# One row of inverse lengths by way of DRAM, and four places for residual tiles, in a two-layer trunk kernel

## The chip, the cores and the metric

The kernel runs on one core of a Trainium2 chip. Its time is the device time of one execution in microseconds. The core has five engines with instruction queues of their own: TensorE (PE; its weight loads are listed apart as PEld), VectorE (DVE), ScalarE (ACT), GpSimd (POOL) and SyncE (SP), which here issues nearly all DMA transfers. Each queue is worked off in order.

## The reference, cut to what matters

The trunk has two layers over 1024 positions of width 1024. The first layer's mixer joins a gated MLP over chunks with a gated delta rule; the second layer's mixer is a differential attention with 8 heads. After its mixer each layer has an MLP and a gated side input. All is in float32.

```python
def rms_norm(x, gain):
    xf = x.astype(jnp.float32)
    y = xf * lax.rsqrt(jnp.mean(xf * xf, axis=-1, keepdims=True) + NORM_EPS)
    return (y * gain.astype(jnp.float32)).astype(x.dtype)

...
        if layer % 2 == 0:
...
            h = h + jnp.concatenate([a_out, b_out], axis=-1) @ w_out_e[i]
        else:
...
            h = h + o @ w_out_o[i]
        hn = rms_norm(h, ln_mlp[layer])
        h = h + jnp.square(jax.nn.relu(hn @ w_mlp1[layer])) @ w_mlp2[layer]
        gate = jax.nn.sigmoid(rms_norm(h, ln_ple[layer]) @ w_ple_gate[layer])
        h = h + (p[layer] @ w_ple_proj[layer]) * gate
```

The change touches two things in this: the factor `rsqrt(mean(...))` of the normalization ahead of the first MLP, for the first half of the positions, and the addition `h + o @ w_out_o` of the second mixer, for the second half of the positions.

## The kernel before

**Layout.** Features lie on the 128 partitions and positions along the free dimension, in two halves of 512 positions (`HT`). The residual stream `h` lies in DRAM (`h_dram`) as eight tiles of 128 features by 1024 positions. Weights are loaded in pieces (`raw`, 8 places), and each piece is split into a high and a low part (`w`, 12 places): ScalarE makes the high part (L230) and VectorE the low part (L234). Each product is three matmuls, high by high, low by high and high by low (`mm3`). A matmul of 128 by 512 adds into one PSUM bank, and a bank is free again when VectorE has added it to its tile.

**Order.** A scheduler orders the instructions of each engine when the program is built, by its own estimate of times. That estimate includes the DMAs, so a step that is made another way can move its neighbours too. Each DMA on SP waits in the queue for what it needs, and all behind it wait too.

**First mixer's end.** `mix_out` multiplies the mixed heads by the output weights, one half of the positions after the other, eight output tiles `m` of 24 matmuls each. For each `m` it adds the bank to the residual tile (`acc`, L1343), adds its square to the running sums (`sqs`, L253 to L257) and stores the tile. After the first half it calls `rms`: four matmuls with a column of ones sum `sqs` over the partitions (tile `aux`), VectorE makes the mean (`ms`, L273) and GpSimd the inverse length `r` (L275), 512 numbers, 4 on each partition. What follows needs them as a row of 512 on every partition (`rb`). `rms` has two ways for that. The near way multiplies `r`, broadcast, by the identity matrix (four matmuls into `aux`, with `r` and `ident` as operands) and copies the bank on ScalarE (L287). The far way stores `r` to DRAM in the order of positions (`rd`, L279) and loads it back to all partitions (L281); three other calls use it. Then VectorE scales each of the eight tiles of the first half with gain and `rb` (L1354), ScalarE casts the high part (`hi`, L1358) and VectorE takes the low part (`lo`, L1359). The MLP's first products read these.

While the first half ends, the second half's last heads are still coming in: four transposes (`pab`, L83) each, then a cast on ScalarE (`ahi`, L1665) and the low part on VectorE (`alo`, L1666). The second half's out-projection reads them.

**Attention's end.** The second mixer's out-projection is made in parts: heads 0 to 5 of the first half of the positions and heads 0 to 4 of the second half are multiplied while the last attention blocks still run (`mix_part`, called for `h` 0 and then 1), and the other heads after the attention (`mix_out` with `k0` 6 and 5). `mix_part` loads a residual tile (`res`, L1298) one output tile ahead, adds the bank (L1310) and stores it back to DRAM (L1311). The tiles `res` take turns in the places `c0` and `c1`. The places `c0` to `c3` hold q tiles of the attention: `c0` and `c1` for even heads, `c2` and `c3` for odd heads, so the last head (7) has `c2` and `c3`. After the last value product of head 7 its two halves are transposed and split (`ohi` L1194, `olo` L1195).

Of the kernel before, what the change touches and what calls it, by code (L numbers as in the profile page):

```python
# [11 lines left out]
F32 = mybir.dt.float32  # L12
# [6 lines left out]
P = 128  # L19
# [4 lines left out]
HT = 512  # L24
# [19 lines left out]
def f32(ap):  # L44
    return ap.bitcast(F32)
# [73 lines left out]
class Trunk:  # L119
# [1170 lines left out]
    def mix_part(self, h, n, w_out, h_dram):  # L1290
        nc = self.nc
        cols = slice(h * HT, (h + 1) * HT)
        res = []

        def load():
            if len(res) < KT:
                res.append(self.slot(f"c{len(res) % 2}", [P, HT], F32, "res"))
                nc.sync.dma_start(res[-1], h_dram[len(res) - 1, :, cols])  # L1298

        load()  # L1300
        for m in range(KT):
            if m % 2 == 0:
                w = self.weight(w_out[0 : n * P, m * P : (m + 2) * P], n, 256)
            load()
            ps = self.mm_ps()
            for k in range(n):
                self.mm3(ps, w.at(k, slice((m % 2) * P, (m % 2 + 1) * P)), self.mixed[h][k], k == 0, k == n - 1)
                if k % 2:
                    yield
            nc.vector.tensor_tensor(res[m], res[m], ps, ALU.add)  # L1310
            nc.sync.dma_start(h_dram[m, :, cols], res[m])  # L1311


    def mix_out(self, h, acc, w_out, h_dram, gain_next, k0=0, late=0):

        nc = self.nc
        cols = slice(h * HT, (h + 1) * HT)
        n = KT - k0
        wide = 256 if n == KT else 512
        pss, place = {}, {}  # L1320

        order = [(m, i) for m in range(KT) for i in range(n)]
        if late:
            order[: 2 * n] = sorted(order[: 2 * n], key=lambda o: (o[1] >= n - late, o))
        for m, i in order:
            ml = m % (wide // P)
            if i == 0:
                if ml == 0:
                    w = self.weight(w_out[k0 * P :, m * P : m * P + wide], n, wide, per=512 // wide)
                a = place[m] = acc(m)  # L1330
                nc.sync.dma_start(a, h_dram[m, :, cols])
                pss[m] = self.mm_ps()
            a, ps = place[m], pss[m]
            k = (i + late) % n
            if h == 1 and k0 and (m, i) == (5, 0):

                self.pe.floor = self.rb_mark
            self.mm3(ps, w.at(k, slice(ml * P, (ml + 1) * P)), self.mixed[h][k0 + k], i == 0, i == n - 1)
            self.pe.floor = None
            if i < n - 1:  # L1340
                yield
                continue
            nc.vector.tensor_tensor(a, a, ps, ALU.add)  # L1343
            self.add_square(h, a)
            nc.sync.dma_start(h_dram[m, :, cols], a)
            yield
        self.sqs_last = self.sqs[h]
        if h == 0:
            self.rb[0] = self.rms(0, self.sqs[0])[1]
            self.rb_mark = self.pe.mark  # L1350
            lows = []
            for m in range(KT):
                a = acc(m)
                inst = nc.vector.scalar_tensor_tensor(a, a, gain_next[:, m : m + 1], self.rb[0], ALU.mult, ALU.mult)  # L1354
                if m > 1:
                    self.pe.behind(inst, lows[m - 2])
                hi, lo = self.hs_new[0][m] = self.hs_parts(0, m)
                nc.scalar.copy(hi, a)  # L1358
                lows.append(nc.vector.tensor_tensor(lo, a, f32(hi), ALU.subtract).ins.name)  # L1359
        yield  # L1360
# [858 lines left out]
```

## Time and profile before

| | us |
|---|---|
| median of 3 executions | 2503.18 (2501.72 to 2505.22) |
| the profiled execution | 2504.11 |
| its span, first to last instruction | 2502.4 |
| TensorE busy in the span | 2491.0 |
| VectorE busy | 1811.0 |
| ScalarE busy | 1312.9 |

The 1.7 us between the profiled execution's time and its span lie around the span. Times in the quoted rows are microseconds from the span's start, with the start first and the length second. In rows of waits, "A <- B" says that A waited for B, with the total, the number of times and the longest. In rows of stretches, each engine's busy time stands with its number of instructions, then the clock granted to TensorE (1.00 is full), the DMA engines' busy share and GB/s.

### The profile page before, as it was taken

The numbers are of one execution on the slowest core, as the hardware profiler recorded it, in microseconds if no ns is written. First come the engines' busy times: TensorE is split into PE (matmuls) and PEld (weight loads), VectorE is DVE, ScalarE is ACT, GpSimd is POOL, SyncE is SP. The second block draws the span as 40 slices with busy tenths as digits, with TensorE's granted clock in tenths as the row PEclk, the third lists the DMA queues.
The fourth block names the chain that finished last, engine by engine and source line by source line (L and its number), as shares of the span: only waits on it lengthen the run. The fifth ranks groups of instructions, "written<-read, shape, count | busy, mean of one in ns | idle before, by whom it ended". The sixth has DMA issues, their size and how long they took to land.

```text
span 2502.4 us, 39882 instructions
## 1 busy us (share of the span) xinstructions
PE 2491.0 (100%) x13905; PEld 2139.8 (86%) x13905; DVE 1811.0 (72%) x3542; ACT 1312.9 (52%) x2669; POOL 284.9 (11%) x267
## 2 busy tenths in 40 slices
PE   9999999999999999999999999999999999999999
PEld 7898998888888888888999999988888888888887
DVE  7868665787666877656577877776887656787576
ACT  6635473555555444534466666654654555445452
POOL 0211220000000000000444444410000000000000
PEclk9999999999999999999999999999999999999999
DMA  8464435467547756543211111367466548656651
GB/s 241 125 185 106 148 125 184 137 208 242 190 160 272 243 165 211 187 134 130 77 56 55 52 52 60 110 209 235 141 219 229 188 166 294 202 189 203 198 177 64
DMA packets 318835, 410.81 MB, mean 164 GB/s; under 512 B 45765, under 2 KB 181929, under 8 KB 318633
## 3 DMA queue, kind: packets, MB, share of 16 engines
q1 hardware_dynamic: 318072, 407.73, 50.8%
q8 instruction: 109, 1.79, 0.3%
q14 instruction: 94, 0.76, 0.1%
q10 hardware_dynamic: 560, 0.53, 0.1%
HBM read 295.95 MB, written 112.20 MB: 163 GB/s over the span
## 4 chain that ended last, share of the span: by engine, by line
PE 96%; DVE 2%; DMA 1%; issue 0%; ACT 0%; POOL 0%; SPq 0%; DVEq 0%; ACTq 0%
PE mm L80 83%; PE po L80 3%; PE qk L80 2%; PE aux L80 2%; PE tr L83 2%; DVE lg L1128 1%; DVE lg L1139 0%; PE pks L80 0%; PE pkq L80 0%; PE pvn L80 0%; PE pkk L80 0%; PE pgm L80 0%; DMA h_dram<-res 0%; PE pab L83 0%; DMA x<-in_x_dram 0%
## 5 line engine op out<-in xcount | busy, mean ns | idle before, releaser
L230 ACT CAST w<-raw 128x512 fp32r<-128x512 f32 x598 | 366.8, 617 | 466.9 <-PE mm L80 411.6
L80 PE MATMUL mm<-g,w 128*128 128x512 f32 x2592 | 601.0, 394 | 0.0
L80 PEld LDWEIGHTS mm<-g,w 128*128 128x128 f32 x2592 | 486.8, 188 | 113.0
L80 PE MATMUL mm<-hi,w 128*128 128x512 f32 x1728 | 554.2, 395 | 0.0
L80 PE MATMUL mm<-w,hi 128*128 128x256 f32 (+2 forms) x2528 | 507.4, 295 | 0.9 <-DVE k L1030 0.9
L234 DVE TENSOR_TENSOR w<-raw,w 128x512 fp32r<-128x512 f32 x534 | 367.3, 694 | 194.6 <-ACT w L230 183.0
L80 PEld LDWEIGHTS mm<-w,hi 128*128 128x128 f32 x2528 | 401.2, 188 | 13.9 <-issue 1.2
L80 PEld LDWEIGHTS mm<-hi,w 128*128 128x128 f32 x1728 | 324.5, 188 | 73.7 <-ACT u L386 0.4
L80 PE MATMUL mm<-w,lo 128*128 128x256 f32 (+2 forms) x1264 | 370.2, 294 | 0.0
L80 PE MATMUL mm<-lo,w 128*128 128x512 f32 x864 | 340.3, 394 | 0.0
L80 PE MATMUL mm<-t,w 128*128 128x512 f32 x1152 | 271.2, 394 | 0.0
L80 PEld LDWEIGHTS mm<-t,w 128*128 128x128 f32 x1152 | 216.5, 188 | 50.5
L80 PEld LDWEIGHTS mm<-w,lo 128*128 128x128 f32 x1264 | 238.2, 189 | 5.5
L80 PEld LDWEIGHTS mm<-lo,w 128*128 128x128 f32 x864 | 162.5, 188 | 36.0
L275 POOL TENSOR_TENSOR r<-ms,mhalf 128x4 f32<-128x4 f32 x12 | 14.1, 1173 | 1507.7 <-DVE ms L273 1478.6
L234 DVE TENSOR_TENSOR g<-graw,g 128x512 fp32r<-128x512 f32 x216 | 147.7, 685 | 6.5 <-DMA gd<-g 5.0
L230 ACT CAST g<-graw 128x512 fp32r<-128x512 f32 x216 | 132.7, 617 | 22.9 <-DMA gd<-g 11.8
L1131 ACT ACTIVATE lg<-lg,nm 128x256 f32<-128x256 f32 (+7 forms) x128 | 99.1, 775 | 69.7 <-DVE nm L1128 67.9
L370 ACT ACTIVATE g<-g 128x512 f32<-128x512 f32 x100 | 63.0, 631 | 82.1 <-DVE g L304 81.8
L1128 DVE CUSTOM_DVE_ANT_0 lg<-qk,al 128x512 f32<-128x512 f32 (+3 forms) x128 | 74.6, 589 | 36.8 <-PE qk L80 32.8
L234 POOL TENSOR_TENSOR w<-raw,w 128x512 fp32r<-128x512 f32 x64 | 84.1, 1332 | 76.3 <-ACT w L230 51.5
L80 PE MATMUL mm<-ohi,w 128*128 128x512 f32 x256 | 85.5, 405 | 2.4 <-DVE res L1310 2.3
(360 smaller groups left out, 3577.5 us busy)
## 6 DMA issues: line engine op xcount, KB each, us to landing
raw<-in_w_mlp_dram SPq DMA_DIRECT2D x352, 256.0 KB, 3.3
graw<-gd SPq DMA_DIRECT2D x224, 256.0 KB, 2.7
gd<-g SPq DMA_DIRECT2D x192, 256.0 KB, 3.3
raw<-in_w_ple_gate_dram SPq DMA_DIRECT2D x76, 256.0 KB, 3.6
acc<-h_dram SPq DMA_DIRECT2D x64, 256.0 KB, 4.8
keep<-in_w_mlp_dram SPq DMA_DIRECT2D x64, 256.0 KB, 4.9
raw<-in_w_in_e_dram SPq DMA_DIRECT2D x60, 256.0 KB, 3.7
h_dram<-acc SPq DMA_DIRECT2D x48, 256.0 KB, 2.7
```

The lines of the kernel that those rows point to most:

```text
L80: self._next(self.engine.matmul(*a, **k))
L83: self._next(self.engine.transpose(*a, **k))
L230: inst = self.nc.scalar.copy(hi, src)
L234: inst = (lo_engine or self.nc.vector).tensor_tensor(lo, src, f32(hi), ALU.subtract)
L275: nc.gpsimd.tensor_tensor(r, ms, self.mhalf[:, 0:4], ALU.pow)
L370: nc.scalar.activation(g, src, AF.Relu)
L1128: nc.vector.tensor_tensor_reduce(out=lg[:, k0:k1], in0=ps[:, : k1 - k0], in1=al[:, u0 + k0 : u0 + k1], scale=-1.0, scalar=3.0e38 if c == 0 ...
L1131: nc.scalar.activation(lg[:, :n], lg[:, :n], AF.Exp, bias=nm[:, r, nch - 1 : nch], scale=-1.0, accum_out=me.sums[:, b, r : r + 1])
```

## The change

`mix_out` asks for the far way where `k0` is 0, that is in the first mixer; the second mixer's call keeps the near way. In `mix_part` the residual tiles of the second half of the positions (`h` 1) take turns in four places, `c0` to `c3`; the first half keeps two.

```diff
@@ mix_part
         def load():
             if len(res) < KT:
-                res.append(self.slot(f"c{len(res) % 2}", [P, HT], F32, "res"))
+                res.append(self.slot(f"c{len(res) % (4 if h else 2)}", [P, HT], F32, "res"))
                 nc.sync.dma_start(res[-1], h_dram[len(res) - 1, :, cols])
@@ mix_out
         if h == 0:
-            self.rb[0] = self.rms(0, self.sqs[0])[1]
+            self.rb[0] = self.rms(0, self.sqs[0], far=not k0)[1]
             self.rb_mark = self.pe.mark
             lows = []
```

What the far way is in `rms`:

```python
        if rows and far:
            d = self.dp.tile([4, P], F32, name=self.nm("rd"))
            nc.sync.dma_start(d.rearrange("t p -> p t"), r)
            rb = self.sp.tile([P, HT], F32, tag=f"rb{half}", name=self.nm("rb"), bufs=1)
            nc.sync.dma_start(rb, d.rearrange("t p -> (t p)").partition_broadcast(P))
```

The scheduler's order moves with it at the first place. Names end in running numbers, which are lower by 3 in the changed kernel from here on, since it has four matmuls and a copy less and two DMAs more. VectorE at the end of the first half, before:

```order
L273 TENSOR_SCALAR ms_4933<-aux_4928 128x4
L234 TENSOR_TENSOR w_5231<-raw_5228,w_5230 128x512
L1354 SCALAR_TENSOR_TENSOR acc_4384<-acc_4384,cols,rb_4942 128x512 x2
L1666 TENSOR_TENSOR alo_5014<-pab_5008,ahi_5013 128x512
L234 TENSOR_TENSOR w_5237<-raw_5234,w_5236 128x512
L1359 TENSOR_TENSOR lo_4946<-acc_4384,hi_4945 128x512
```

And VectorE at the same place now, up to the addition that empties the first bank of the second half:

```order
L273 TENSOR_SCALAR ms_4933<-aux_4928 128x4
L1666 TENSOR_TENSOR alo_5011<-pab_5005,ahi_5010 128x512
L1354 SCALAR_TENSOR_TENSOR acc_4384<-acc_4384,cols,rb_4939 128x512 x2
L1666 TENSOR_TENSOR alo_5029<-pab_5023,ahi_5028 128x512
L1359 TENSOR_TENSOR lo_4943<-acc_4384,hi_4942 128x512
...
L234 TENSOR_TENSOR w_5234<-raw_5231,w_5233 128x512
L1343 TENSOR_TENSOR acc_5077<-acc_5077,mm_5079 128x512
```

The first `alo` moved ahead of the two L1354, which read the row `rb`; the second `alo` now follows right behind them (it came after two more of them and two splits before), and the weights' split `w_5228` moved behind them. Between the second `alo` and the L1343 stand ten instructions: four L1359, four L1354 and two L234.

TensorE at the same place, before:

```order
L80 MATMUL aux_4928<-ones,sqs_4484 128x1 x4
...
L80 MATMUL aux_4937<-ident,r_4935 128x128 x4
L83 MATMUL pab_5008<-ident,qkv_2756 128x128 x4
...
L83 MATMUL pab_5026<-ident,qkv_2756 128x128 x4
```

And now, where 18 matmuls stand between the two sets of transposes, 27 between the second set and the first reader of `alo_5029`, and 22 from that reader to the first matmul into `mm_5251`, whose bank is the one that `mm_5079` had:

```order
L80 MATMUL aux_4928<-ones,sqs_4484 128x1 x4
L83 MATMUL pab_5005<-ident,qkv_2756 128x128 x4
...
L83 MATMUL pab_5023<-ident,qkv_2756 128x128 x4
...
L80 MATMUL mm_5079<-alo_5029,w_5073 128x512
...
L80 MATMUL mm_5251<-ahi_4724,w_5227 128x512
```

The four matmuls with `r` are gone, the first transposes moved up to the sums, and a part of the fourth output tile's matmuls moved behind the first reader of `alo_5029`.

SP at the same place now:

```order
L105 DMA raw_5330<-in_w_out_e_dram 128x2x256
L279 DMA rd_4937<-r_4935 128x4x1
L281 DMA rb_4939<-rd_4937 128x512
L1331 DMA acc_5249<-h_dram 128x512 x4
L352 DMA raw_5461<-in_w_mlp_dram 128x2x256
```

The two DMAs stand behind the last weight tile of the out-projection; the MLP's first weight tile (`in_w_mlp`) came ahead of the four residual loads before.

SP at the attention's end, before; the last residual tile is `res_19093`:

```order
L1298 DMA res_19035<-h_dram 128x512
L1331 DMA acc_19364<-h_dram 128x512
L1311 DMA h_dram<-res_18997 128x512
L105 DMA raw_19434<-in_w_out_o_dram 128x512
L1298 DMA res_19055<-h_dram 128x512
L1331 DMA acc_19237<-h_dram 128x512 x4
L1331 DMA acc_19446<-h_dram 128x512
L105 DMA raw_19440<-in_w_out_o_dram 128x512
L1311 DMA h_dram<-res_19035 128x512
L352 DMA raw_19574<-in_w_mlp_dram 128x2x256
L1311 DMA h_dram<-res_19055 128x512
L1298 DMA res_19093<-h_dram 128x512
```

And now, where the last residual tile is `res_19090` and the store four tiles before it is that of `res_18953`:

```order
L1298 DMA res_19052<-h_dram 128x512
L105 DMA raw_19355<-in_w_out_o_dram 128x512
L1311 DMA h_dram<-res_18953 128x512
L1331 DMA acc_19361<-h_dram 128x512
L105 DMA raw_19425<-in_w_out_o_dram 128x512
L1298 DMA res_19090<-h_dram 128x512
L1331 DMA acc_19361<-h_dram 128x512
L1311 DMA h_dram<-res_18994 128x512
```

The load of the last residual tile moved ahead of the stores of the three tiles before it. The orders of TensorE and VectorE are the same there before and now.

## The prediction

> **What bounds the kernel now.** I read the page, then what TensorE waits for, then the chain of work that ended last at the two places of the change, then each engine's instructions there in order of time.
>
> ```profile
> PE 2491.0 (100%) x13905; PEld 2139.8 (86%) x13905; DVE 1811.0 (72%) x3542; ACT 1312.9 (52%) x2669; POOL 284.9 (11%) x267
> ...
> PE 96%; DVE 2%; DMA 1%; issue 0%; ACT 0%; POOL 0%; SPq 0%; DVEq 0%; ACTq 0%
> ```
>
> TensorE is busy for 2491.0 of 2502.4 us. A microsecond by which TensorE is put off is a microsecond of the kernel; what another engine gains is worth nothing unless TensorE waits for it. Its waits:
>
> ```profile
> PE mm L80 <- DVE res L1310: 2.3, 1, 2.3
> ...
> PE mm L80 <- DVE acc L1343: 0.2, 1, 0.2
> ```
>
> The first, its longest in the program, lies at the second place (residual tiles); the second is the only one at the first place (inverse lengths). So the second edit has something to win; the first has almost nothing to win and must not open a wait.
>
> **First edit: the row by way of DRAM.** The chain at the place, from the sums of squares (`aux`, 423.55) on:
>
> ```profile
> 423.55 0.79 PE aux L80 x8
> 424.34 5.89 PE mm L80 x25
> 430.23 0.89 PE aux L80 x8
> 431.12 0.44 PE pab L83 x4
> ...
> 433.39 4.90 PE mm L80 x21
> ...
> 441.91 29.25 PE mm L80 x125
> ```
>
> TensorE never stands still: a matmul starts every 0.2345 us (5.89 for 25, 4.90 for 21). Removed: the four broadcasting matmuls, 0.89 us of TensorE (the row at 430.23), and the copy that followed on ScalarE, which lies beside TensorE and saves nothing. The other engines:
>
> ```profile
> 425.16 1.01 POOL L275 TENSOR_TENSOR r<-ms,mhalf 128x4 f32<-128x4 f32 x1 [58.94 <-DVE ms L273]
> ```
> ```profile
> 431.78 1.42 DVE L1354 SCALAR_TENSOR_TENSOR acc<-acc,cols,rb 128x512 f32<-128x512 f32 x2 [1.04 <-ACT rb L287]
> ...
> 436.18 0.75 DVE L1354 SCALAR_TENSOR_TENSOR acc<-acc,cols,rb 128x512 f32<-128x512 f32 x1
> 436.84 0.69 DVE L1666 TENSOR_TENSOR alo<-pab,ahi 128x512 fp32r<-128x512 f32 x1
> 437.44 0.68 DVE L234 TENSOR_TENSOR w<-raw,w 128x512 fp32r<-128x512 f32 x1
> ```
>
> GpSimd has r at 426.17 and VectorE uses the row at 431.78, 5.6 us later. (Between starts on VectorE: 0.66 us after an L1354, 0.60 after the others.) Added: two DMAs on SP, r to DRAM and back to all partitions. Three other places of this kernel do the same, and one shows it undisturbed:
>
> ```profile
> 1109.43 1.01 POOL L275 TENSOR_TENSOR r<-ms,mhalf 128x4 f32<-128x4 f32 x1 [41.71 <-DVE ms L273]
> ```
> ```profile
> 1110.46 0.37 SPq L279 DMA_DIRECT2D rd<-r  x1
> 1118.92 0.34 SPq L281 DMA_DIRECT2D rb<-rd  x1
> ```
> ```profile
> L279 SPq DMA_DIRECT2D rd<-r x3: 366/370/387, 39.8 to 1110.5; - x3
> ...
> DMA to landing us min/median/max: 8.4/8.4/8.4
> ```
> ```profile
> L281 SPq DMA_DIRECT2D rb<-rd x3: 320/338/339, 50.4 to 1118.9; - x3
> ...
> DMA to landing us min/median/max: 5.5/5.5/5.5
> ```
>
> The first DMA lands 8.4 us after its issue and the second 5.5, at all three places alike; here the second leaves 8.46 after the first. So r at 426.2 gives the second DMA at 434.65, the row at 440.15, and the first L1354 at 440.2: 14.0 us after r, and 8.4 later than before.
>
> What queues behind that wait: on VectorE, in order, the two L1354 and then the lower part of the last transposed head (`alo`, L1666), which the out-projection reads. It starts at 440.2 + 2 x 0.66 = 441.5 and ends 0.69 later, at 442.2. TensorE has, between the sums (end 424.34) and its first use of that tile, two sets of four transposes (0.44 each) and by the new order 18 and 27 matmuls: 424.34 + 0.88 + 45 x 0.2345 = 435.8. There it stops for 6.4 us.
>
> Then come 22 matmuls (5.2 us: 447.4) up to the first into a new PSUM bank, which VectorE has to empty first (L1343). In the new order `alo`, four L1359 and two L234 (0.60 each) and four L1354 (0.66 each) start ahead of that L1343: 441.5 + 6.84 = 448.4, its end 449.05. So that matmul starts at 449.1 instead of 441.91: **+7.2 us**, the 0.89 counted in. A slower clock after the gap (below) takes some 1.5 us from those 22 matmuls, which then end at 448.9, still under the same wait.
>
> Two queues more. SP stands from 426.2 to 434.65: the four residual loads behind it leave at 435 (before: 433.5) and are first used after 24 more matmuls, past 454; the MLP's first weight tile waits for its place until VectorE's split at 445 (before: issued at 430.8) and is used after the 96 matmuls left of this projection, at 449.1 + 22.5 = 471.6. Both have 10 us and more to spare. On ScalarE the next weight cast moves behind two `hi` casts, to 442.3; that is inside the VectorE chain above. Nothing later gives the 7.2 us back, because from 441.91 on the chain before is TensorE alone.
>
> **Second edit: four residual tiles.**
>
> ```profile
> 1725.13 6.67 DMA h_dram<-res
> 1731.81 0.02 issue
> 1731.82 2.92 DMA res<-h_dram
> ```
> ```profile
> 1712.68 0.38 SPq L1311 DMA_DIRECT2D h_dram<-res  x1
> ...
> 1717.44 0.32 SPq L1298 DMA_DIRECT2D res<-h_dram  x1
> ```
> ```profile
> 1729.82 0.69 DVE L234 TENSOR_TENSOR w<-raw,w 128x512 fp32r<-128x512 f32 x1 [0.70 <-PE mm L80]
> 1734.87 0.69 DVE L1310 TENSOR_TENSOR res<-res,mm 128x512 f32<-128x512 f32 x1 [4.35 <-DMA res<-h_dram]
> ```
> ```profile
> 1732.86 0.40 PE L80 MATMUL mm<-ohi,w 128*128 128x512 f32 x1
> 1735.61 0.79 PE L80 MATMUL mm<-ohi,w 128*128 128x512 f32 x1 [2.35 <-DVE res L1310]
> ...
> 1738.97 0.63 PE L80 MATMUL mm<-ohi,w 128*128 128x512 f32 x2
> ```
> ```profile
> 1735.00:1736.00 1.00, 0.39 (x1) 0.39 (x2) 1.00 (x2) 0.00 (x0) 0.00 (x0) 0.64 0.80 252
> 1736.00:1737.00 1.00, 1.00 (x3) 0.77 (x3) 1.00 (x3) 0.00 (x0) 0.00 (x0) 0.50 0.87 270
> 1737.00:1738.00 1.00, 1.00 (x4) 0.75 (x3) 1.00 (x2) 0.55 (x1) 0.00 (x0) 0.50 1.04 379
> 1738.00:1739.00 1.00, 1.00 (x5) 0.79 (x4) 0.44 (x2) 0.67 (x2) 0.00 (x0) 0.65 1.01 365
> 1739.00:1740.00 1.00, 1.00 (x6) 0.83 (x5) 1.00 (x3) 0.72 (x2) 0.00 (x0) 1.00 0.98 372
> ```
>
> The last residual tile takes the place of the one two before it, so its load waits for a store that lands 6.67 us after its issue. VectorE's addition waits for the load (4.35 us), and TensorE for the bank that this addition empties. With four places the load waits only for the store four tiles back (issued 1712.68), and in the new order it stands ahead of the next store, at about the place of the 1717.44 load: landed long before VectorE is free at 1730.4. The bank is then empty at 1731.1 and TensorE goes on at 1733.1.
>
> The gain is more than the 2.35 us of waiting, since the granted clock (the third figure from the right, in slices of 1 us) is at 0.50 for 0.72 + 2 + 0.70 = 3.4 us after the gap and 1.00 again at 1739. By counting: between 1732.86 and 1738.97 nine matmuls start, in 6.11 us instead of 9 x 0.2345 = 2.11: **-4.0 us**. The Trainium skill, "TensorE: Matmul & The Clock Gate", section "Why this matters for your kernels", asks for no TensorE gaps above about 3 us; by it this 2.35 us gap would leave the clock alone, and the sum below would be +4.8. The row at 0.50 decides against that.
>
> The extra places held the last head's q tiles; their last transposes are done before either load is due, and no DMA wait on SP grows. VectorE's and TensorE's orders are unchanged here. Late next would be the bank behind it, freed by the `olo` two instructions later on VectorE, at 1732.4, before its matmul at 1734.5. The other loads of this part leave earlier, which nothing uses.
>
> **Sum.** +7.2 - 4.0 = +3.2 us on the profiled execution's 2504.11, 0.9 above the median of 2503.18; against the median 2506.4, which I round to **2506.5**. 0.2%, or 5.0 us, is about what a measurement of this kernel can tell from no change.
>
> **Rivals.**
>
> *Faster.* One mechanism: a short round trip. The shortest frequent DMA here:
>
> ```profile
> graw<-gd SPq DMA_DIRECT2D x224, 256.0 KB, 2.7
> ```
>
> Two at 2.7 us give the row at 431.6, as early as now. TensorE then meets no wait, 0.89 + 0.16 are saved at the first place and 4.0 at the second: 2498.1. It decides from a row at 433.7 on (no gap); the two edits cancel with a row at 437.0. Against it stand the three equal landings at 8.46 and 5.5: 512 single words written apart, unlike a 256 KB tile. Chance 0.06. The Trainium skill, "DMA: Bandwidth & Descriptors", section "Anatomy of one DMA — SWDGE (gpsimd) path", gives about 2.0 us fixed per DMA (for the GpSimd path, where this queue is SP's); an estimate from it, 4 us for both, would put the row at 430.2, the same case. The trace's 14.0 us speaks against it.
>
> *Slower by more than 5 us.* The clock after the 6.4 us gap stays at half for two stretches of 3.4 us (the length seen at the second place). Then the 22 matmuls lose 3.4 us, not 1.5, and end at 450.8: +8.9 - 4.0 = +4.9; half a microsecond more in the DMAs makes it 2508.9. Or SP's order at the second place brings another late load and only the 2.35 us, or nothing, comes back: +4.8 to +7.2, up to 2510.4. For it: the gap is nearly three times the one seen; against it: one stretch was enough there. Chance 0.36.
>
> *The edits do nothing.* The new order has the two DMAs and the early loads; no chance of its own.
>
> **How the numbers follow.** My forecast, within 0.2%, has 0.58: +2 to +5, from 7.2 to 8.2 at the first place and 3.5 to 5.2 at the second (the 2.35 us of waiting, and a clock at half for 2 to 5.4 us, an estimate: 0.6 to 1.6 stretches of 3.4, since the gap may end anywhere in one). The range adds the scatter of the executions before (2501.7 to 2505.2) below and the slower case above: 2502.5 to 2510.5.
>
> **What would show it.** Right: rb leaves SP 8.5 us after rd near 434.7; TensorE stands about 6.4 us near 436, released by `alo` L1666, with a granted clock of 0.5 behind it; the wait for `res` L1310 near 1735 is gone and the clock stays 1.00 there. Wrong: no gap near 436 (a short round trip), a gap well over 7 us, or TensorE waiting near 1735 again.

## The result, and the profile after

| | before | now |
|---|---|---|
| median | 2503.32 (16 executions, 2501.72 to 2506.73) | 2509.00 (16 executions, 2507.55 to 2510.44) |
| the profiled execution | 2504.11 | 2507.87 |
| its span | 2502.4 | 2506.2 |

All in us. The ratio is 1.0021, with a 95% interval of 1.0015 to 1.0027. That is slower, by about as much as a measurement of this kernel can tell. It lies 2.5 us above the forecast of 2506.5.

TensorE's waits in the changed kernel (in total, times, longest):

```profile
PE mm L80 <- DVE alo L1666: 5.4, 1, 5.4
...
PE aux L80 <- DVE ms L273: 0.3, 1, 0.3
PE mm L80 <- DVE w L234: 0.3, 1, 0.3
```

The wait for `res` (L1310) is gone. A wait for `alo`, more than twice as long, has come. The chain of work at the first place:

```profile
424.82 1.02 POOL r L275
425.84 0.02 issue
425.86 7.54 DMA rd<-r
...
433.46 5.53 DMA rb<-rd
438.99 0.02 issue
439.02 1.41 DVE acc L1354 x2
440.43 0.61 DVE alo L1666
441.05 0.04 issue
441.09 36.41 PE mm L80 x147
477.50 0.56 PE aux L80 x6
```

GpSimd's r is there at 425.84, the row on all partitions at 438.99: 13.2 us for the trip. Then come two scalings and the low part that was queued behind them, and only then TensorE. The clock granted to TensorE there (third figure from the right, stretches of 2 us):

```profile
438.00:440.00 2.00, 0.00 (x0) 0.00 (x0) 0.98 (x2) 0.20 (x1) 0.00 (x0) 0.68 1.01 365
440.00:442.00 2.00, 0.91 (x2) 0.82 (x3) 2.00 (x4) 1.56 (x3) 0.00 (x0) 0.50 0.36 139
442.00:444.00 2.00, 2.00 (x6) 1.52 (x6) 2.00 (x4) 1.02 (x2) 0.00 (x0) 0.50 0.00 0
444.00:446.00 2.00, 2.00 (x7) 1.54 (x6) 2.00 (x5) 1.28 (x4) 0.00 (x0) 0.61 0.28 79
446.00:448.00 2.00, 2.00 (x10) 1.63 (x9) 2.00 (x5) 1.82 (x5) 0.00 (x0) 1.00 0.15 52
```

At half clock for 1.28 + 2 + 2 + 1.56 = 6.8 us, of which TensorE works only from 441.09 on. The second place, on VectorE and in the same view:

```profile
1736.71 0.68 DVE L1310 TENSOR_TENSOR res<-res,mm 128x512 f32<-128x512 f32 x1
```
```profile
1736.00:1738.00 2.00, 2.00 (x13) 1.64 (x12) 1.90 (x4) 1.38 (x3) 0.00 (x0) 1.00 0.85 313
```

The last L1310 follows the split ahead of it without idle time, and the clock stays at 1.00.

To see where the time went, I cut each profiled execution at three moments that every kernel has: TensorE's first matmul of the sums at the end of the first mixer's first half (A), the same at the end of its second half (B), and the first such matmul at the end of the second mixer's first half (C). In us, worked out from the starts of those matmuls:

| kernel | A to B | B to C | C to the end |
|---|---|---|---|
| before | 47.61 | 1284.57 | 746.84 |
| now | 53.91 | 1280.56 | 748.27 |
| difference | +6.30 | -4.01 | +1.43 |

A to B holds the first place, B to C the second. The third column was in no term of the forecast.

### The profile page after: what moved, and what is told of

Read it like the earlier page. It is cut to its first block, busy times and chain, and to the rows that moved or that the text cites. A ratio compares the mean times of both kernels' runs of the same rounds, so it can differ in the third digit from the quotient of the medians.

```text
span 2506.2 us, 39867 instructions
## 1 busy us (share of the span) xinstructions
PE 2492.6 (99%) x13897; PEld 2139.0 (85%) x13897; DVE 1808.8 (72%) x3542; ACT 1313.6 (52%) x2668; POOL 285.3 (11%) x267
## 4 chain that ended last, share of the span: by engine, by line
PE 94%; DVE 3%; DMA 2%; issue 1%; ACT 0%; POOL 0%; SPq 0%; DVEq 0%; ACTq 0%
PE mm L80 81%; PE po L80 3%; PE qk L80 2%; PE aux L80 2%; PE tr L83 2%; DMA raw<-in_w_ple_gate_dram 1%; DVE lg L1128 1%; DVE lg L1139 0%; DMA h_dram<-xt 0%; DMA rd<-r 0%; DVE w L234 0%; PE pks L80 0%; PE pkq L80 0%; PE pkk L80 0%; PE pvn L80 0%
## 5 line engine op out<-in xcount | busy, mean ns | idle before, releaser
L234 DVE TENSOR_TENSOR w<-raw,w 128x512 fp32r<-128x512 f32 x534 | 365.6, 691 | 194.3 <-ACT w L230 184.0
L234 DVE TENSOR_TENSOR g<-graw,g 128x512 fp32r<-128x512 f32 x216 | 147.2, 683 | 5.3 <-DMA gd<-g 5.2
L234 POOL TENSOR_TENSOR w<-raw,w 128x512 fp32r<-128x512 f32 x64 | 84.1, 1333 | 76.5 <-ACT w L230 51.6
L80 PE MATMUL mm<-ahi,w 128*128 128x512 f32 x256 | 84.0, 405 | 0.2 <-ACT ahi L1665 0.2
```

Of the source, the lines that this page charges most:

```text
L80: self._next(self.engine.matmul(*a, **k))
L234: inst = (lo_engine or self.nc.vector).tensor_tensor(lo, src, f32(hi), ALU.subtract)
```

## The experiments

The medians stand against those of the kernel before on the same chip: 2502.74 for the first four, 2503.04 for the next four, 2504.24 for the last two.

### One edit at a time

```diff
@@ row_only: the kernel before, with
-            self.rb[0] = self.rms(0, self.sqs[0])[1]
+            self.rb[0] = self.rms(0, self.sqs[0], far=not k0)[1]
@@ places_only: the kernel before, with
-                res.append(self.slot(f"c{len(res) % 2}", [P, HT], F32, "res"))
+                res.append(self.slot(f"c{len(res) % (4 if h else 2)}", [P, HT], F32, "res"))
@@ three_places: as places_only, with
+                res.append(self.slot(f"c{len(res) % (3 if h else 2)}", [P, HT], F32, "res"))
```

> The first edit alone: the row goes by DRAM in the first mixer, the residual tiles keep two places. The theory of the prediction: the trip of some 13 us holds VectorE's queue at the end of the first mixer's first half, TensorE waits 5 to 6.5 us there for the second low part (alo) behind the two scalings, and part of what follows runs at half clock; +7 us against the kernel before, 2510.3 (2508.5 to 2512), with the wait of 2.3 us on res and its stretch of half clock still there at the attention's end. Rival 1, the changed kernel's 2.5 us over the forecast lie at this place: +9.5 us, 2512.8. Rival 2, the second edit brings nothing in the timed runs: the same as the changed kernel, 2509.

> The second edit alone: four places for the second half's residual tiles, the row on the near way. The theory of the prediction: the wait on res and the half clock behind it go, nothing else moves: -4.0 us against the kernel before, 2499.3 (2498 to 2500.5), and the trace shows no stretch of half clock ahead of the last one. Rival 1, the changed kernel's 2.5 us over the forecast lie at this place (a later wait takes back what is won): 2501.8. Rival 2, it brings nothing in the timed runs: 2503.3.

> The near way, and three places (c0 to c2) for the second half's residual tiles. The theory of the prediction: a load has to be one output tile further ahead of the store that frees its place, and no more, to take away a wait of 2.3 us: as with four places, 2500.1 (2499 to 2501). Rival, the store's landing of 6.7 us and the load need the fourth place too: a wait on res stays, 2501.5 to 2503.

| kernel | median | against before | ratio, 95% interval | A to B | B to C | C to the end |
|---|---|---|---|---|---|---|
| row_only | 2513.50 | +10.8 | 1.0045 (1.0032 to 1.0058) | 54.46 | 1285.44 | 747.62 |
| places_only | 2500.11 | -2.6 | 0.9989 (0.9981 to 0.9998) | 47.61 | 1280.53 | 746.76 |
| three_places | 2500.40 | -2.6 | 0.9986 (0.9977 to 0.9995) | 47.60 | 1280.50 | 746.92 |

The traces bear out both places: 6.85 us lost between A and B with the row alone, 4.04 won between B and C with the places alone. Three places do what four do: the load has to be one tile further ahead, no more. The waits of `row_only`:

```profile
PE mm L80 <- DVE alo L1666: 5.2, 1, 5.2
PE mm L80 <- DVE res L1310: 3.0, 1, 3.0
```

But by the medians the places are worth 2.6 us, not the 4.0 expected, and the row alone costs 10.8: 2513.50 lies above the expected range, which ended at 2512, and above its first rival's 2512.8. A part of the answer lies in the kernel before. Each execution is listed with its mean granted clock. Of the 27 executions of before on the first chip, 20 list 1.000, with a median of 2502.47, and 7 list 0.999, with 2505.46; on the second chip 19 (2502.48) and 8 (2505.22), on the third 9 (2502.86) and 10 (2504.66). A stretch of 3.4 us at half clock lowers the mean over 2502 us by 0.0007, which just shows in the third digit. The profiled execution of before lists 0.999, and its trace has that stretch behind the wait for `res`. So the execution from which I took -4.0 is of the rarer kind. Against the 1.000 kind the places win 2502.47 - 2500.11 = 2.4 us, which is the wait of 2.35 alone; against the profiled execution 2504.11 - 2500.11 = 4.0, as its trace says. All executions of `places_only` and `three_places` list 1.000. Against the median of the rarer kind the gain is 5.4 us, and that is more than the clock explains: 3.4 us at half clock cost at most half of that, 1.7, and the two kinds lie 3.0, 2.7 and 1.8 us apart on the three chips. What else parts them isn't shown; the wait's length in the executions without a trace isn't known.

The profiled execution of `row_only` lost the clock at both places. Against the common execution of before, taken as 1280.53 + 2.4 between B and C, it loses 6.85 us between A and B, 1285.44 - 1280.53 - 2.4 = 2.5 between B and C and 0.8 behind, 10.1 of the 11.0 that part 2513.50 from 2502.47. How often its other executions lost the clock at the second place can't be read from the lists: they show 0.998 and 0.997, and the changed kernel, whose trace loses it at the first place alone, lists 0.998 too in 7 of 16 executions.

### What makes TensorE wait at the first place

In `row_together` the row is stored in the order in which r lies, four words of each partition side by side, for this call alone, and read with a stride. In `scale_later` and `scale_behind_low` the eight scalings, their casts and low parts become a function of their own, and its first two scalings are ordered behind a given instruction:

```diff
@@ mix_out
-            lows = []
-            for m in range(KT):
...
+            self.scale = lambda mark: self.scaled(acc, gain_next, mark)
+            if k0:
+                self.scale(None)
@@ scale_later: mix_out, behind an output tile's addition
+            if h == 1 and not k0 and m == 1:
+                self.scale(added.ins.name)
@@ scale_behind_low: even_mix, at the end, with the name of the last alo
         for _ in put_b(1):
             pass
+        self.scale(self.alo)
@@ row_together: rms and mix_out
-            d = self.dp.tile([4, P], F32, name=self.nm("rd"))
-            nc.sync.dma_start(d.rearrange("t p -> p t"), r)
+            d = self.dp.tile([P, 4] if flat else [4, P], F32, name=self.nm("rd"))
+            nc.sync.dma_start(d if flat else d.rearrange("t p -> p t"), r)
...
+                if not k0:
+                    rb = self.rb[0].rearrange("p (q t) -> p t q", t=4)
```

> Both edits, but the eight scalings with the row (and the casts and low parts made of them) are issued later, behind the addition that empties the second half's second bank, so that VectorE has nothing in its queue that waits for the row. Theory 1, TensorE stands still only because alo and the bank's addition are queued behind the scalings, and the trip itself hides: no wait on alo, no half clock there, and the four matmuls with r are saved (0.89 us): 2503.3 - 4.0 - 0.9 = 2498.4 (2497 to 2500). Theory 2, the row is wanted so early that the wait moves to the MLP's first products or to the accumulation tiles: TensorE waits later for hi or lo, 2503 or more.

> Both edits, but the eight scalings stand on VectorE behind the second alo alone, and still ahead of the addition that empties the second half's first bank. Theory 1, every entry behind the scalings pays for the trip: TensorE no longer waits for alo, but for the bank (L1343), which comes after four scalings, three low parts and two splits, some 5.5 us after rb lands: about 4 us of waiting and a stretch of half clock, 2503 to 2506. Theory 2, alo was the one wait that mattered: 2499 to 2500.5, as with the scalings issued later.

> Both edits, but r is stored as it lies, four words of a partition side by side, and loaded to all partitions in that order; the scaling then reads the row with a stride of four words. The order of all engines is the changed kernel's. Theory 1, the store takes 7.5 us because it is 512 single words: with 128 pieces it lands in 2 to 4 us, rb comes 3.5 to 5.5 us earlier, TensorE's wait for alo falls from 5.4 us to between 0 and 2, and the time by 4 to 7 us against the changed kernel, to 2502 to 2505. Theory 2, the time of the trip does not hang on the number of pieces: rb lands at the same moment, 2509. A slower scaling through the strided reading (over its 0.65 us) would give a part of the gain back at the bank's addition behind it.

| kernel | median | against before | ratio, 95% interval | A to B | C to the end |
|---|---|---|---|---|---|
| scale_later | 2499.72 | -3.0 | 0.9987 (0.9978 to 0.9996) | 46.31 | 747.68 |
| scale_behind_low | 2508.55 | +5.5 | 1.0018 (1.0009 to 1.0027) | 54.66 | 748.56 |
| row_together | 2506.39 | +3.7 | 1.0014 (1.0005 to 1.0023) | 52.36 | 748.46 |

VectorE in `scale_later`:

```profile
436.35 1.28 DVE L1343 TENSOR_TENSOR acc<-acc,mm 128x512 f32<-128x512 f32 x2 [0.22 <-PE mm L80]
439.41 1.41 DVE L1363 SCALAR_TENSOR_TENSOR acc<-acc,cols,rb 128x512 f32<-128x512 f32 x2 [1.77 <-DMA rb<-rd]
```

The row lands as late as in the changed kernel (439.4 against 439.0), VectorE even stands idle for it, and TensorE doesn't notice: what it needs, `alo` and the emptied banks, was done ahead. A to B is 1.3 us shorter than in the kernel before, 0.89 of it the four matmuls. So the trip itself can be hidden; its price in the changed kernel is what stands behind the scalings in VectorE's queue. In `scale_behind_low` only `alo` was taken out of that line:

```profile
PE mm L80 <- DVE acc L1343: 5.6, 1, 5.6
```
```profile
439.40 1.41 DVE L1361 SCALAR_TENSOR_TENSOR acc<-acc,cols,rb 128x512 f32<-128x512 f32 x2 [8.27 <-DMA rb<-rd]
...
445.84 1.28 DVE L1343 TENSOR_TENSOR acc<-acc,mm 128x512 f32<-128x512 f32 x2
```

The next in line pays instead: the bank's addition stands 6.4 us behind the first scaling, and TensorE waits 5.6 us for it. I had expected some 4 us of waiting and 2503 to 2506; the place is right, the price was too low.

In `row_together` the store takes 3.3 us instead of 7.5, and the load 4.05 instead of 5.5:

```profile
426.77 3.27 DMA rd<-r
...
430.11 4.05 DMA rb<-rd
434.16 0.03 issue
434.19 2.18 DVE acc L1357 x2
...
437.49 1.13 DVE acc L1357
```
```profile
PE mm L80 <- DVE acc L1343: 3.1, 1, 3.1
...
PE mm L80 <- DVE alo L1669: 0.9, 1, 0.9
```

The row is there 5 us earlier and the wait for `alo` falls to 0.9, as the first theory said. But each scaling that reads the row with a stride takes 1.13 us, not 0.75, and the bank's addition behind the chain comes late: 3.1 us of waiting. The median lies 2.6 us under the changed kernel's (2.0 when each is taken against the kernel before on its own chip), not the 4 to 7 expected.

### The trip without anybody waiting for the row

```diff
@@ near_and_trip: places_only, with, in rms at the first place
             nc.scalar.copy(rb, pb)
+            if half == 0 and sqs is getattr(self, "sqs_last", 0) and not self.k0:
+                d = self.dp.tile([4, P], F32, name=self.nm("rd"))
+                nc.sync.dma_start(d.rearrange("t p -> p t"), r)
+                nc.sync.dma_start(self.tmp(), d.rearrange("t p -> (t p)").partition_broadcast(P))
```

> Four places, the row on the near way, and beside it r stored to DRAM and loaded to all partitions into a tile that nothing reads. Theory 1 on the trip, it costs only what waits for it: 2500.1, as with the four places alone. Rival, its 512 single words and its two places in SP's queue hold up the loads behind them: 2501 or more, with TensorE waiting near 440 us. On the second layer's MLP: 585.36 us if the missing matmuls set its pace, 586.35 us if the row's DMAs do.

2509.73 us, +5.5 (1.0022, 1.0012 to 1.0032), where the theory had 2500.1: the rival. The chain:

```profile
425.67 7.62 DMA rd<-r
...
433.70 4.81 DMA t<-in_diff_lambda_dram
438.50 0.02 issue
438.53 0.23 DVE t L971
...
439.28 0.58 ACT rb L287
```
```profile
PE pab L83 <- ACT rb L287: 6.9, 1, 6.9
```

The load of the attention's constants came to stand behind the two DMAs on SP. VectorE waits for it, ScalarE waits for VectorE, and the copy that frees the bank for TensorE's transposes stands behind that on ScalarE. In the changed kernel that load is ahead of the trip. So on SP's queue it went as on VectorE's: the trip cost what stood behind it and was wanted soon.

### The 1.4 us behind the second mixer

From the chain of before, of now and of `near_and_trip`, the second layer's MLP, TensorE alone:

```profile
1785.24 291.91 PE mm L80 x1260
...
2078.90 283.18 PE mm L80 x1224
```
```profile
1787.65 292.17 PE mm L80 x1260
...
2081.57 283.91 PE mm L80 x1224
```
```profile
2083.38 283.18 PE mm L80 x1224
```

As many matmuls, no gap, and yet 0.26 and 0.73 us more. I take the stage from the last matmul of the sums over the partitions at the second mixer's end to the first of those at the MLP's end (first half of the positions). It takes 585.35 us before and 586.36 now, and this is no scatter: 585.35 to 585.38 in before, `places_only`, `three_places` and `near_and_trip`; 586.33 to 586.36 in now, `row_only`, `row_together`, `scale_later` and `scale_behind_low`. Single matmuls start mostly at intervals of 226 to 242 ns, and which of them is long or short is the same in two kernels of one group to about 1 ns. Three kernels ask for the cause; `IDLE` is the number of unread matmuls at the program's start, and each of them, like each of the four with r, makes two matmul records in the trace:

```diff
@@ scale_later_idle: scale_later, with
-IDLE = 6
+IDLE = 10
@@ before_idle2: the kernel before, with
-IDLE = 6
+IDLE = 2
@@ later_and_matmuls: scale_later, with, in rms behind the row's load
+            if half == 0 and sqs is self.sqs_last:
+                pb = self.aux_ps()
+                for t in range(4):
+                    self.pe.matmul(pb[:, t * P : (t + 1) * P], lhsT=r[:, t : t + 1].to_broadcast([P, P]), rhs=self.ident, start=True, stop=True)
+                nc.scalar.copy(self.tmp(), pb)
```

> The kernel with the scalings issued later, with four matmuls more among the unread ones at the program's start (10 in place of 6, each two matmul records of the trace), so that from the first mixer's end on TensorE's queue has as many instructions ahead of it as in the kernel before. The second layer's MLP, from the row's matmuls to the sums of its end (2540 matmuls), took 585.35 and 585.38 us in the two kernels on the near way and 586.34 to 586.36 us in the four on the far way. Theory 1, the matmul's pace hangs on where an instruction stands in TensorE's queue: 585.36 again, and about 1 us less in all, 2498.7, if the start does not grow. Theory 2, it hangs on the row's DMAs or buffers: 586.35 again, 2499.7 or a little more.

> The kernel before with four matmuls less among the unread ones at the start (2 in place of 6): no row by DRAM, two places. Theory 1 on the second layer's MLP, the number of instructions ahead sets its pace: 586.35 us in place of 585.36. Theory 2, the row's DMAs or buffers set it: 585.36 as before.

> The kernel with the scalings issued later, and beside the row by DRAM the near way's four matmuls with r and the copy of their bank on ScalarE, which nothing reads. TensorE has all matmuls of the kernel before again. Theory 1, the missing matmuls ahead are what set the pace of the second layer's MLP: 585.36 us in place of 586.35, and 0.9 us more at the place itself: 2499.6 in all. Theory 2, the row's two DMAs or the tile rd do it: 586.35, 2500.6.

| kernel | matmul records ahead of the stage | row by DRAM | the stage |
|---|---|---|---|
| before, near_and_trip | 10726 | no; beside it | 585.35, 585.38 |
| now, scale_later | 10718 | yes | 586.36, 586.35 |
| scale_later_idle | 10726 | yes | 586.00 |
| later_and_matmuls | 10726 | yes | 586.08 |
| before_idle2 | 10718 | no | 584.95 |

Neither theory holds. The row's DMAs are not the cause: `near_and_trip` has them at 585.38, and `before_idle2` moves the stage without them. The count of matmuls ahead is not enough either: 10726 of them go with three values. What all the kernels with another value share is another stream of matmuls ahead on TensorE (the unread matmuls also move the order at the program's start). But another order does not always come with another value: the matmuls of now and of `scale_later` stand in another order between 441 and 466 us, and their values agree to 0.01 us. How that reaches a stage 1300 us later stays open.

As times these three say little: `scale_later_idle` takes 2501.90 (0.9992, 0.9983 to 1.0001), with 3.5 us of new waiting for weights at the longer start; `before_idle2` 2514.5 in one execution, 10 us of it lost in the first 80 us; `later_and_matmuls` 2504.92 (1.0006, 0.9997 to 1.0015), and in it too the load of the attention's constants slipped behind the trip, so that TensorE waited 2.2 us for `alo`. The first and the last lie above what either of their theories had given (about 2499.7 and 2500.6 at most).

The other 0.4 us: near 2414 TensorE stands 0.3 us for `ms` (L273), and the chain behind that leads back to late weight tiles of the last stage. Such a wait for `ms` is in now (0.3), `row_together` (0.5), `scale_behind_low` (0.7) and `scale_later_idle` (0.6), and in none of the others; what decides it wasn't tried.

## Why the prediction was right and wrong

**Right: the wait at the first place.** The chain is the one worked out: store, load, two L1354, `alo`, TensorE. The load took 5.53 us against 5.5. The store let SP go on after 7.6 us, not the 8.46 that I took from a later place; over the kernels it was 7.3 to 8.1 here. So the gap is 5.36 us, not 6.4:

```profile
441.09 0.79 PE L80 MATMUL mm<-alo,w 128*128 128x512 f32 x1 [5.36 <-DVE alo L1666]
```

SP's later loads cost nothing here, as argued.

**Wrong in a detail there: the half clock does not hide as a whole.** I put the slow matmuls under the wait for the bank (L1343). That wait never came, as these rows of VectorE and of TensorE show:

```profile
447.21 1.28 DVE L1343 TENSOR_TENSOR acc<-acc,mm 128x512 f32<-128x512 f32 x2
```
```profile
448.11 0.63 PE L80 MATMUL mm<-ahi,w 128*128 128x512 f32 x2
```

The first of the two additions is over near 447.9, the end of VectorE's work without idle time from 439.02 on. The new bank's first matmul, 22 behind the one at 441.09, is the second of the two in the other row, at 448.3; TensorE comes there without a gap. At full clock the 22 would have ended at 441.09 + 22 x 0.2345 = 446.2, and TensorE would have stood for the bank until 447.9. So by an estimate from these rows the slow clock took 2.1 us from the 22 matmuls; 1.7 of them are hidden as argued, and 0.4 are not. The slow clock is two stretches long, as in the slower rival. The rival's price was too high all the same, because 2.4 us of the first stretch passed while TensorE stood. Both sizes together: +6.3 instead of +7.2.

**The term that failed: -4.0 at the second place.** The mechanism is right, and between the two profiled executions the gain is 4.01 us. But most executions of the kernel before list no lost clock. Against them the gain is 2.4 us, and by all medians 2.6, below the 3.5 to 5.2 that I gave the term (its own parts, 2.35 and half of 2 to 5.4, make 3.4 to 5.1). I took a term that depends on the clock from one execution, though the range of the three shown (2501.72 to 2505.22) was nearly as wide as the term. This is some 1.5 us of the miss, and it is what the slower rival said of the second place: only the wait comes back. The rule weighed there, of no TensorE gaps above about 3 us (the Trainium skill, "TensorE: Matmul & The Clock Gate", section "Why this matters for your kernels"), would fit those executions, if their gap was as long, which no trace shows; the profiled one speaks against it, since its gap of 2.35 us was followed by half clock.

**Not foreseen:** 1.0 us of slower pace in the second layer's MLP, and 0.4 us in the last stage. Neither was a term or a rival. With the places' gain by all medians the sum is then 6.3 - 2.6 + 1.4 = +5.1; measured are +5.7. The 0.6 us left over have no account; the profiled execution of the changed kernel, from which 6.3 and 1.4 come, lies 1.1 us below the median of its 16.

**The rivals.** A short round trip is out: 13.2 us. Of the slower case both halves came about in part, the two stretches and the smaller gain at the second place, and the result, +5.7 us, lies just above the 5.0 that divide it from the forecast. That 2509.0 is inside the range is owed to the room left for this rival and for scatter, and not to the sum. The 0.9 us that the first place cost less than forecast paid for a part of what the second place and the unforeseen 1.4 us added, and that is luck.

The gain to be had is the places alone: 2500.11, or 2500.40 with three. With the scalings moved the row by DRAM does no harm, but its 2499.72 can't be told from 2500.11: what it saves between A and B it loses in the MLP's pace.

## What to carry to other kernels

A round trip through DRAM cost nothing here by its length where nothing was queued behind it (`scale_later`), and 4.8 us and more between A and B by what was queued behind its first reader or behind its DMAs. Look for the first instruction after each that the engine which bounds the kernel wants, and move the reader behind all of them, since taking out one only handed the wait to the next (`scale_behind_low`). When a term holds a stretch of lower clock, ask how many executions show it before it goes into the sum. Shortening a transfer by another layout has to be paid wherever the layout is read.

## What the runs showed of the hardware

- **The clock changes on a grid.** In the trace's clock records the full clock lasts whole multiples of 3.413 us: 507 of them before the first stretch at half in the kernel before, 127 in the changed kernel, and each stretch within the program at half is one or two. The Trainium skill, "TensorE: Matmul & The Clock Gate", section "What's actually happening", gives windows of 3413 ns that run freely; the records agree, with the grid starting at the first full clock, 4.7 to 9.9 us into the span. A gap of TensorE of 2.18 us that filled 0.64 of one such window (`later_and_matmuls`) was followed by a window at half, and so was 2.35 us that filled 0.59 of one in before; a gap of 2.13 us that a border split into 0.48 and 0.15 (`scale_later_idle`) was not. That would explain why a gap of this length costs the clock in some executions and not in others; it is not shown, since only profiled executions have such records.
- **Single words are dear to store.** 512 words stored one by one land after 7.5 us, and the same 2 KB in pieces of four words after 3.3 us.
- **A stride in one operand costs VectorE.** The scaling takes 1.13 us with the row read at a stride of four words, and 0.75 us without.
- **The pace of back-to-back matmuls is a property of the program.** The same 2540 matmuls took 584.95 to 586.36 us in twelve kernels, and the same to 0.03 us in kernels of one group; what sets it stays open.
